# The start, one pair's Gram products and the last square root of a streaming-encoder block on Trainium2

## The chip, the cores and the metric

The kernel runs on one core of one Trainium2 chip. Time is device time in microseconds of that core, from launch to end; the profiled execution also has a span, from its first to its last instruction. Five engines matter: TensorE (PE, and PEld for its weight loads), VectorE (DVE), ScalarE (ACT), GpSimd (POOL) and SyncE (SP), which only issues transfers. Each runs its own list of instructions in order and waits for the others by semaphores.

## The reference

512 frames of 2048 features, ahead of them 16 learned meta tokens, pass one block. An RMS norm and one input projection `P = hn @ w_in` (2048 columns to 8320) feed two groups: sixteen heads of an RWKV-7 recurrence, and a gated convolution of width 3. Both are gated, put together, multiplied by `w_out` and added to the input; a last RMS norm gives the output.

```python
hn = _rmsnorm(h_res, norm_in_g[l])
P = hn @ w_in[l]
...
w_raw = -jax.nn.softplus(-(w0[l] + jnp.tanh(wl) @ w_lora_up[l])) - 0.5
decay = jnp.exp(-jnp.exp(w_raw.astype(jnp.float32)))
...
S = (S * w_t[:, :, None, :] - sa[..., None] * b_t[:, :, None, :]
     + v_t[..., None] * k_t[:, :, None, :])
y_t = jnp.einsum('bhvk,bhk->bhv', S, r_t)
...
h_res = h_res + mix @ w_out[l]
out = _rmsnorm(h_res, norm_f_g)
```

## The kernel before, in words

**Precision.** A product of float32 matrices is made of three matmul passes. Each operand is cut into a high part of reduced width (`xh`, `hi`) and the rest (`xl`, `lo`): high by high, high by rest, rest by high. ScalarE makes the high part (a cast or a scaled copy), VectorE or POOL subtracts it to get the rest. So each 128x512 piece of weights costs a cast (L134) and a subtraction (L135) before TensorE can use it, and each 128-row block of x costs the same with the norm's gain folded in (`split_x`, L207 and L208).

**The projection.** `plan` lists 65 column tiles of `w_in`: lora, k, r, v, g, and for the convolution B, C, h, gc. Features lie on the 16 blocks of 128 partitions (`kt`), and frames are the matmul's columns, 528 of them in two banks of PSUM (256 and 272; 258 where only the 512 real frames and two before them are wanted; one bank of 512 for B and gc). A main matmul is one pass of one block into one bank (L328).

**The head.** Nothing can start before the first weights and the first block of x have come. So the first four tiles (lora, k, r, B) are computed side by side, block by block: for each of the first four blocks (a step) TensorE goes through lora, k, r and B. For this the host packs one array, `front`, in the order in which the pieces are used; four transfers bring it (L237). The first holds the gain, lora's weights of block 0 and block 0 of x; the second k, r and B of block 0; the third the four weights and x of block 1; the fourth blocks 2 and 3. Later loads follow on the same SP queue: the second half of the first weights (`load_w`, L221), then x in groups (`load_x`, L201). A transfer waits until one of eight semaphore lanes is free, so at most eight are under way. Scratch tiles of later stages serve as landing places (`in_bt`, `in_r`, `in_bk`, `in_gt`). Before the first data come, TensorE multiplies zeros (`pwarm`, L187: two float32 matmuls of 512 columns, each of which shows as two passes).

**Fillers.** TensorE's list is written out by hand. `mains()` is a generator that issues the main matmuls of the plan, and everything else calls `fill(ns)` to draw that much main work between two of its own groups, so that the answers of other engines and of transfers come back while TensorE does main work. The numbers are in the table `FW`. `later(ns, ...)` puts a transfer into the list when that much main work has been drawn. The other engines' lists come from a scheduler, except in stretches marked as manual (the head on VectorE and ScalarE, and the end).

**Pairs.** Two heads form a pair; `prepare(i)` handles pair i, and two pairs at a time go through `invert`. In `prepare`, `gram` (L682) multiplies keys by queries for each of nine chunks of frames; the results stand in PSUM as `za` (chunks 0 to 3), `zc` (4 to 7) and `ze` (chunk 8), one bank for each head. `za` lies in the pool `tz`, `zc` in `misc` and `ser`, and `ze` in the pool `main`, which the main matmuls use too. `masked` (L692) multiplies each bank by a mask on VectorE into `gt`, and thereby frees the bank. After a fill (`gram2`) come the sums `n2` and `zb` (L713 to L717). `recur` then goes through the nine chunks; its operands come back from DRAM as `ct` (`load_chunk`), and its first matmuls are `rz` (L957). The fill ahead of it is `begin`.

**The end.** The output projection works with sums of blocks of the mix (units P, M, Q, L1242). Its last unit, M2 of the second half, is done in three pieces: 512 columns for rows 0 to 127, and two of 256 for rows 128 to 255 (L1449). For each 128 rows the sum of squares is collected by ScalarE (L1229, then a read of the accumulator), `row_scale` makes the factor from it, and `finish` scales and stores. The factor is (sum + eps) to the power -0.5: an addition and then a power on POOL (L98). `finish_last(1)` handles the last rows on three engines at once.

Of the kernel before, what the change touches and what calls it, by code (L numbers as in the profile page):

```python
# [9 lines left out]
F32 = mybir.dt.float32  # L10
# [3 lines left out]
ALU = mybir.AluOpType  # L14
# [30 lines left out]
    tr=3200, lev=3000, cp=4200, out=1500, begin=20300, p=2900, u=2900, s=4800, last=3700, mix=2600,  # L45
# [32 lines left out]
def hymba_kernel(ctx: ExitStack, tc: tile.TileContext, xt, xtok, front, w_in, w_out, pv, lup, cst, msk, gf, out):  # L78
# [104 lines left out]
    cold = tp.tile([P, 512], F32, tag="tm", name="cold", bufs=3)  # L183
    nc.vector.memset(cold, 0.0)
    pwarm = pi.tile([P, 512], F32, tag="ser", name="pwarm")
    for _ in range(2):
        nc.tensor.matmul(pwarm, cold[:, 0:P], cold, start=True, stop=True)  # L187
# [17 lines left out]
    def split_x(kt, cols=slice(0, L)):  # L205
        gain = ng[:, kt : kt + 1]
        nc.scalar.activation(xh[:, kt, cols], raw[kt][:, cols], AF.Copy, scale=gain)  # L207
        return nc.vector.scalar_tensor_tensor(  # L208
            out=xl[:, kt, cols], in0=raw[kt][:, cols], scalar=gain, in1=xh[:, kt, cols].bitcast(F32),
            op0=ALU.mult, op1=ALU.subtract,  # L210
        ).ins

    def square_x(kt, first=False):
        sq = accd if first else tr(f"sqx{kt}")[:, 0:L]
        nc.scalar.activation(sq, raw[kt], AF.Square)
        if not first:
            nc.vector.tensor_tensor(out=accd, in0=accd, in1=sq, op=ALU.add)
# [12 lines left out]

    for n in range(4):
# [3 lines left out]
    o = 0  # L235
    for t in fr:
        nc.sync.dma_start(t, front[:, o : o + t.shape[1]])  # L237
        o += t.shape[1]
    ng = fr[0]
    raw[0], raw[1] = fr[0][:, KT + P : F0], fr[2][:, 4 * P : F1]  # L240
    for k in range(2):
        raw[2 + k] = fr[3][:, 8 * P + k * L : 8 * P + (k + 1) * L]
# [3 lines left out]
    nc.scalar.activation(warm, warm, AF.Tanh)  # L246
# [4 lines left out]
    with tc.manual_schedule(engines={mybir.EngineType.DVE, mybir.EngineType.Activation}):  # L251
        split_piece(0, 0, fr[0][:, KT : KT + P])
        split_x(0, slice(0, L // 2))
        split_x(0, slice(L // 2, L))
        for n in (1, 2, 3):
            split_piece(n, 0, fr[1][:, (n - 1) * P : n * P])
        split_x(1)
        for n in range(4):
            split_piece(n, P, fr[2][:, n * P : (n + 1) * P])
        for kt in (2, 3):  # L260
            split_x(kt)
            if kt == 2:
                for n in range(4):
                    split_piece(n, 2 * P, fr[3][:, 2 * n * P : 2 * (n + 1) * P])
# [48 lines left out]
    HALF = SEQ // 2  # L313
# [169 lines left out]
    def mains():  # L483
# [5 lines left out]
        for k in range(4):  # L489
            for n, (ps, rg) in enumerate(four):  # L490
                if k == n == 0:
                    hi, lo = quarters[0]
                    for ww, xx, first in ((hi, xh, True), (lo, xh, False), (hi, xl, False)):
                        for p, (a, b) in zip(ps, rg):
                            nc.tensor.matmul(p, ww[:, 0:P], xx[:, 0, a:b], start=first, stop=False)
# [131 lines left out]
    def prepare(i):  # L627
# [799 lines left out]
    with tc.manual_schedule(engines={mybir.EngineType.DVE, mybir.EngineType.Activation, mybir.EngineType.Pool}):  # L1427
# [3 lines left out]
        for t in (2, 3):  # L1431
            row_part(t, 3)
            row_scale(t, 3)
        row_part(0, 3)
# [25 lines left out]
        row_scale(1, 4, nc.vector)  # L1460
        gain(1, 2, nc.vector, slice(256, 512))
        finish_last(1)


def _layout(i):
# [35 lines left out]
    front += [t[:, 1] for t in first] + [xt[:, 1]] + [t[:, 2:4].reshape(P, 256) for t in first] + [xt[:, 2], xt[:, 3]]  # L1501
# [24 lines left out]
```

## Time and profile before

| | us |
|---|---|
| median of the runs (3; 999.9 to 1000.47) | 1000.18 |
| the profiled execution | 999.89 |
| its span | 998.0 |
| TensorE busy | 986.7 |
| VectorE busy | 689.2 |
| ScalarE busy | 412.2 |
| POOL busy | 271.6 |
| first real matmul (L495) starts | 4.63 |
| last group of matmuls (L1449) ends | 990.1 |

In rows of the order of time the first number is the start in us from the start of the span, the second the duration; then come engine, line, operation, what is written from what, shape and count, and in brackets idle time of the engine before it and what ended it. In rows of a tile the three numbers are the shortest, the median and the longest duration in ns. Matmuls overlap in their pipeline, so the distance between two starts says more than a duration. The loads of data are 139 MB read from HBM over the span, and the data engines are close to full in the first 25 us.

### The profile page before, as it was taken

The page shows a single profiled execution, that of the slowest core. Times are in us where ns is not written, and L with a number is a line of the kernel's source. Part 1 is how long each engine was busy: PE and PEld are TensorE (multiplying, and loading weights), DVE is VectorE, ACT ScalarE, POOL GpSimd, SP SyncE. Part 2 cuts the span into 40 slices and gives each one's busy share as a digit, 9 for nine tenths or more (in the row PEclk, how much of TensorE's full clock was granted, in tenths as well). Part 3 has the DMA queues.
Part 4 walks back from the last instruction along what each step waited for, and adds up shares of the span by engine and source line. Part 5 has one row for each costly group of instructions (what it writes and reads, how often), then busy time and mean ns, then how long its engine had stood idle before and what let it go on. Part 6 is the DMA issues. An engine that isn't in the chain of part 4 may idle for free.

```text
span 998.0 us, 22792 instructions
## 1 busy us (share of the span) xinstructions
PE 986.7 (99%) x9211; PEld 910.8 (91%) x9211; DVE 689.2 (69%) x1314; ACT 412.2 (41%) x770; POOL 271.6 (27%) x286
## 2 busy tenths in 40 slices
PE   9999999999999999999999999999999999999996
PEld 8999999999998999998999998989889898888885
DVE  7777975487774579735579735246555598999895
ACT  7554432343523535232534232233332326645553
POOL 0122423133422324222324222223242423011001
PEclk9999999999999999999999999999999999999999
DMA  9527585437584365854265954978783698798634
GB/s 324 160 79 184 122 224 144 119 106 179 128 215 140 95 180 130 230 145 111 85 180 120 232 143 114 347 266 283 223 266 96 169 266 232 230 293 224 144 99 168
DMA packets 184985, 179.48 MB, mean 180 GB/s; under 512 B 112176, under 2 KB 141616, under 8 KB 184368
## 3 DMA queue, kind: packets, MB, share of 16 engines
q1 hardware_dynamic: 182288, 169.12, 58.2%
q0 software_dynamic: 2304, 8.39, 4.8%
q8 instruction: 72, 1.18, 0.5%
q10 hardware_dynamic: 288, 0.52, 0.1%
q14 instruction: 33, 0.27, 0.1%
HBM read 139.28 MB, written 38.71 MB: 178 GB/s over the span
## 4 chain that ended last, share of the span: by engine, by line
PE 95%; DMA 2%; DVE 1%; issue 1%; POOL 0%; ACT 0%; DVEq 0%; SPq 0%; POOLq 0%
PE ps_g L328 9%; PE ps_r L328 9%; PE ps_h L328 9%; PE ps_gc L328 9%; PE ps_B L328 9%; PE ps_v L328 9%; PE ps_C L328 8%; PE ps_k L328 8%; PE M L1242 8%; PE P L1242 4%; PE Q L1242 2%; PE g L682 2%; DMA ct<-opd 1%; PE ps_lora L328 1%; PE rz L957 1%; PE zs L1004 1%
## 5 line engine op out<-in xcount | busy, mean ns | idle before, releaser
L134 ACT CAST w<-wr 128x512 fp32r<-128x512 f32 x252 | 153.4, 619 | 280.0 <-PE ps_h L328 47.4
L135 POOL TENSOR_TENSOR w<-wr,w 128x512 fp32r<-128x512 f32 x119 | 168.2, 1415 | 365.2 <-ACT w L134 326.7
L135 DVE TENSOR_TENSOR w<-wr,w 128x512 fp32r<-128x512 f32 x133 | 98.3, 743 | 98.6 <-ACT w L134 97.6
L328 PE MATMUL ps_r<-xh,w 128*128 128x256 f32 (+1 forms) x512 | 95.2, 282 | 1.0 <-DVE gt L692 1.0
L328 PE MATMUL ps_k<-xh,w 128*128 128x256 f32 (+1 forms) x512 | 95.4, 284 | 0.0
L328 PE MATMUL ps_v<-xh,w 128*128 128x272 f32 (+1 forms) x512 | 95.4, 284 | 0.0
L328 PE MATMUL ps_h<-xh,w 128*128 128x258 f32 (+1 forms) x512 | 93.1, 281 | 0.0
L328 PE MATMUL ps_C<-xh,w 128*128 128x258 f32 (+1 forms) x512 | 92.5, 281 | 0.0
L328 PE MATMUL ps_g<-xh,w 128*128 128x258 f32 (+1 forms) x512 | 91.7, 280 | 0.0
L328 PE MATMUL ps_B<-xh,w 128*128 128x512 f32 x256 | 83.1, 394 | 0.0
L328 PEld LDWEIGHTS ps_r<-xh,w 128*128 128x128 f32 x512 | 80.2, 189 | 1.6 <-DVE gt L692 1.2
L328 PE MATMUL ps_gc<-xh,w 128*128 128x512 f32 x256 | 81.6, 393 | 0.0
L328 PEld LDWEIGHTS ps_k<-xh,w 128*128 128x128 f32 x512 | 80.3, 189 | 0.3
L328 PEld LDWEIGHTS ps_v<-xh,w 128*128 128x128 f32 x512 | 80.1, 189 | 0.3
L328 PEld LDWEIGHTS ps_h<-xh,w 128*128 128x128 f32 x512 | 79.5, 189 | 0.3
L328 PEld LDWEIGHTS ps_C<-xh,w 128*128 128x128 f32 x512 | 79.2, 189 | 0.6
L328 PEld LDWEIGHTS ps_g<-xh,w 128*128 128x128 f32 x512 | 79.2, 189 | 0.2
L328 PE MATMUL ps_k<-xl,w 128*128 128x256 f32 (+1 forms) x256 | 73.0, 285 | 0.0
L328 PE MATMUL ps_v<-xl,w 128*128 128x256 f32 (+1 forms) x256 | 72.5, 283 | 0.0
L328 PE MATMUL ps_h<-xl,w 128*128 128x256 f32 (+1 forms) x256 | 72.5, 283 | 0.0
L328 PE MATMUL ps_g<-xl,w 128*128 128x256 f32 (+1 forms) x256 | 72.4, 283 | 0.0
L328 PE MATMUL ps_r<-xl,w 128*128 128x256 f32 (+1 forms) x256 | 72.1, 282 | 0.0
(312 smaller groups left out, 2204.3 us busy)
## 6 DMA issues: line engine op xcount, KB each, us to landing
wr<-in_w_in_dram SPq DMA_DIRECT2D x126, 512.0 KB
ct<-opd SPq DMA_DIRECT2D x56, 320.0 KB
wo<-in_w_out_dram SPq DMA_DIRECT2D x21, 512.0 KB
opd<-gt SPq DMA_DIRECT2D x16, 576.0 KB
x<-in_w_out_dram POOLq DMA_DIRECT2D x16, 512.0 KB, 5.7
opd<-ar SPq DMA_DIRECT2D x8, 576.0 KB
opd<-bt SPq DMA_DIRECT2D x64, 64.0 KB
ct<-opd SPq DMA_DIRECT2D x16, 256.0 KB
```

Of the source, the lines that this page charges most:

```text
L134: nc.scalar.copy(hi, rq)
L135: low[q] = eng.tensor_tensor(out=lo, in0=rq, in1=hi.bitcast(F32), op=ALU.subtract).ins
L328: nc.tensor.matmul(ps[r], ww[:, w], xx[:, kt, a:b], start=(kt == 0 and n == 0), stop=(kt == KT - 1 and n == 2))
L682: nc.tensor.matmul(z[h][:, c - c0], bk[hs, c, h : h + 2, :].rearrange("p a s -> p (a s)"), ar[hs, c].rearrange("p a s -> p (a s)"), start= ...
L957: nc.tensor.matmul(z[e][ho if e else hs, 0, k], ct[e][hs, k, o : o + CH], uv(e, k, hs, h) if part else st[hs, 4 * e + k], start=(part == 0 ...
L1004: nc.tensor.matmul(zs[hs, j], bb[:, h], uv(e, k, everything, h), start=True, stop=True)
L1242: nc.tensor.matmul(bank[s], left(prod, jj, m, s), w, start=(jj == 0 and n == 0), stop=(jj == 7 and n == 2))
```

## The change

Five things change.

1. Warming: four matmuls of 128 columns instead of two of 512, on a tile of 128 columns.
2. The front: five transfers instead of four. The first holds the gain, lora's weights and the first 256 columns of block 0 of x; the second the other 272 columns and the weights of k, r and B; then one transfer for each of blocks 1, 2 and 3. The landing places of the first two change (`in_r` for the first, `in_bt` for the second). The fourth and all later loads are held until the first has landed: POOL copies one column from it into the fourth's landing place. Lora's cast of block 0 goes from ScalarE to VectorE, and lora's six passes go by part of x (three passes into the first bank, three into the second) instead of by kind of pass.
3. Gram: for pair 2 chunk 8 comes first, on TensorE as in the masks' program order; for other pairs nothing moves.
4. Two fills are longer: `gram2` of pair 1 by 400 ns and `begin` by 500 ns.
5. The factor of the last rows is a square root on ScalarE and a reciprocal on VectorE; a square root of one unused element stands earlier on ScalarE, so that the table is loaded there. Rows 128 to 255 have their last product with the final gain moved ahead of it.

The first instructions of TensorE, before and after (`ps_lora` has two numbered banks; `w` is the weight slot):

```order
L187 MATMUL pwarm<-cold 128x512 x2
L495 MATMUL ps_lora_331<-xh,w_143 128x256
L495 MATMUL ps_lora_332<-xh,w_143 128x272
L495 MATMUL ps_lora_331<-xh,w_143 128x256
L495 MATMUL ps_lora_332<-xh,w_143 128x272
L495 MATMUL ps_lora_331<-xl,w_143 128x256
L495 MATMUL ps_lora_332<-xl,w_143 128x272
L328 MATMUL ps_k_0_333<-xh,w_144 128x256
```

After:

```order
L187 MATMUL pwarm<-cold 128x128 x4
L506 MATMUL ps_lora_344<-xh,w_145 128x256 x2
L506 MATMUL ps_lora_344<-xl,w_145 128x256
L506 MATMUL ps_lora_345<-xh,w_145 128x272 x2
L506 MATMUL ps_lora_345<-xl,w_145 128x272
L339 MATMUL ps_k_0_346<-xh,w_146 128x256
```

The bank of the second 272 columns is now used only after the first bank is through. SP's first loads, before and after:

```order
L237 DMA in_bt<-in_front_dram 128x672
L237 DMA in_r_148<-in_front_dram 128x384
L237 DMA in_bk<-in_front_dram 128x1040
L237 DMA in_gt_150<-in_front_dram 128x2080
L221 DMA in_g<-in_w_in_dram 128x512
L201 DMA in_gt_157<-in_xt_dram 128x2112
```

After; the fourth waits for POOL, and the others stand behind it:

```order
L242 DMA in_r_150<-in_front_dram 128x400
L242 DMA in_bt<-in_front_dram 128x656
L242 DMA in_bk<-in_front_dram 128x1040
L242 DMA in_gt_149<-in_front_dram 128x1040 x2
L222 DMA in_g<-in_w_in_dram 128x512
L201 DMA in_gt_162<-in_xt_dram 128x2112
```

The first three transfers carry the same 2096 columns, cut at another place. VectorE at pair 2, around the masks (`g2_8_0` is chunk 8 of the first head, `g2_0_1` chunks 0 to 3 of the second):

```order
L821 STREAM_TRANSPOSE vs2_3136<-v2_2781 128x576
L135 TENSOR_TENSOR w72_2858<-wr36_2856,w72_2858 128x512
L692 TENSOR_TENSOR gt2_2919<-g2_0_0_2920,cs_119 128x512
L692 TENSOR_TENSOR gt2_2919<-g2_0_1_2921,cs_119 128x512
L692 TENSOR_TENSOR gt2_2919<-g2_4_0_2922,cs_119 128x512
L692 TENSOR_TENSOR gt2_2919<-g2_8_0_2924,cs_119 128x128
L692 TENSOR_TENSOR gt2_2919<-g2_4_1_2923,cs_119 128x512
L692 TENSOR_TENSOR gt2_2919<-g2_8_1_2925,cs_119 128x128
L352 TENSOR_TENSOR pr_k3_2969<-ps_k3_0_2801,rs_112 128x256
```

After:

```order
L836 STREAM_TRANSPOSE vs2_3153<-v2_2794 128x576
L135 TENSOR_TENSOR w72_2871<-wr36_2869,w72_2871 128x512
L703 TENSOR_TENSOR gt2_2936<-g2_8_0_2941,cs_119 128x128
L703 TENSOR_TENSOR gt2_2936<-g2_8_1_2942,cs_119 128x128
L703 TENSOR_TENSOR gt2_2936<-g2_0_0_2937,cs_119 128x512
L703 TENSOR_TENSOR gt2_2936<-g2_0_1_2938,cs_119 128x512
L703 TENSOR_TENSOR gt2_2936<-g2_4_0_2939,cs_119 128x512
L703 TENSOR_TENSOR gt2_2936<-g2_4_1_2940,cs_119 128x512
L363 TENSOR_TENSOR pr_k3_2982<-ps_k3_0_2814,rs_112 128x256
```

The two small masks move from the fourth and sixth place to the first two. The diff, with the parts left out that only follow from it:

```diff
-    tr=3200, lev=3000, cp=4200, out=1500, begin=20300, p=2900, u=2900, s=4800, last=3700, mix=2600,
+    tr=3200, lev=3000, cp=4200, out=1500, begin=20800, p=2900, u=2900, s=4800, last=3700, mix=2600,
...
-    cold = tp.tile([P, 512], F32, tag="tm", name="cold", bufs=3)
+    cold = tp.tile([P, P], F32, tag="tm", name="cold", bufs=3)
...
-    for _ in range(2):
-        nc.tensor.matmul(pwarm, cold[:, 0:P], cold, start=True, stop=True)
+    for _ in range(4):
+        nc.tensor.matmul(pwarm, cold, cold, start=True, stop=True)
...
-    F0, F1, F2 = KT + P + L, 4 * P + L, 8 * P + 2 * L
-    fr = [view("bt", F0), view("r0", 3 * P), view("bk", F1), view("gt0", F2)]
+    F0, F1 = KT + P + HALF, 4 * P + L
+    X0 = L - HALF
+    two = view("gt0", 2 * F1)
+    fr = [view("r0", F0), view("bt", X0 + 3 * P), view("bk", F1), two[:, 0:F1], two[:, F1 : 2 * F1]]
...
+    for n in range(3):
+        load_front(n)
...
+    nc.scalar.activation(warm, warm, AF.Tanh)
+    nc.gpsimd.tensor_copy(fr[3][:, 0:1], ng[:, 0:1])
+    load_front(3)
+    load_front(4)
...
-        split_piece(0, 0, fr[0][:, KT : KT + P])
-        split_x(0, slice(0, L // 2))
-        split_x(0, slice(L // 2, L))
+        hi, lo = (t[:, 0:P] for t in quarters[0])
+        w0 = fr[0][:, KT : KT + P]
+        nc.vector.tensor_copy(hi, w0)
+        nc.vector.tensor_tensor(out=lo, in0=w0, in1=hi.bitcast(F32), op=ALU.subtract)
+        for cols, t in x0:
+            split_x(0, cols, t)
...
-                    for ww, xx, first in ((hi, xh, True), (lo, xh, False), (hi, xl, False)):
-                        for p, (a, b) in zip(ps, rg):
+                    for p, (a, b) in zip(ps, rg):
+                        for ww, xx, first in ((hi, xh, True), (lo, xh, False), (hi, xl, False)):
...
-        for c in range(NCH):
-            gram((za, zc, ze)[c // 4], c, c // 4 * 4)
-        for z, a, b in ((ze, 8, 9), (za, 0, 4), (zc, 4, 8)) if i == 2 else ((za, 0, 4), (zc, 4, 8), (ze, 8, 9)):
+        blocks = [(za, 0, 4), (zc, 4, 8), (ze, 8, 9)]
+        if i == 2:
+            blocks = blocks[2:] + blocks[:2]
+        for z, a, b in blocks:
+            for c in range(a, b):
+                gram(z, c, a)
+        for z, a, b in blocks:
             masked(z, a, b)
-        fill(FW["gram2"] - shift + 1300 * (i == 1) + 2000 * (i == 3))
+        fill(FW["gram2"] - shift + 1700 * (i == 1) + 2000 * (i == 3))
...
+        if eng is nc.scalar:
+            eng.activation(v, ssq[:, t, n : n + 1], AF.Sqrt, bias=w)
+            nc.vector.reciprocal(r, v)
+            scales[t] = r
+            return
...
+        nc.scalar.activation(fv[:, 1, 1:2], fv[:, 3, 0:1], AF.Sqrt)
...
-        row_scale(1, 4, nc.vector)
         gain(1, 2, nc.vector, slice(256, 512))
+        row_scale(1, 4, nc.scalar)
         finish_last(1)
```

More of the change, by code (lines that the diff above doesn't have):

```diff
@@ L214, in square_x @@
         sq = accd if first else tr(f"sqx{kt}")[:, 0:L]
-        nc.scalar.activation(sq, raw[kt], AF.Square)
+        for cols, t in ((slice(0, L), raw[kt]),) if kt else x0:
+            nc.scalar.activation(sq[:, cols], t, AF.Square)
         if not first:
@@ L245, in hymba_kernel @@
     later_w += [load_w(1, "xT1"), load_w(2, "e1"), load_w(3, "xT0")]
-    nc.scalar.activation(warm, warm, AF.Tanh)
     load_x("ar", 8, 2)
@@ L261, in hymba_kernel @@
             split_x(kt)
-            if kt == 2:
-                for n in range(4):
-                    split_piece(n, 2 * P, fr[3][:, 2 * n * P : 2 * (n + 1) * P])
+            for n in range(4):
+                split_piece(n, kt * P, fr[kt + 1][:, n * P : (n + 1) * P])
         split_w(1, later_w[0], nc.vector)
@@ L1500, in _layout @@
     front = [pv[:, V_NG : V_NG + KT], first[0][:, 0], xt[:, 0]] + [t[:, 0] for t in first[1:]]
-    front += [t[:, 1] for t in first] + [xt[:, 1]] + [t[:, 2:4].reshape(P, 256) for t in first] + [xt[:, 2], xt[:, 3]]
+    for k in range(1, 4):
+        front += [t[:, k] for t in first] + [xt[:, k]]
     front = np.concatenate(front, 1)
```

29 lines of the change are left out of this document (14 added, 15 removed).

## The prediction

> **What bounds the kernel now.** I read the page first (busy times and the chain), then the waits of TensorE, then the order of time at the four places that the change touches. TensorE is busy almost throughout, and the chain that ended last is TensorE for 95 parts in 100.
>
> ```profile
> PE 986.7 (99%) x9211; PEld 910.8 (91%) x9211; DVE 689.2 (69%) x1314; ACT 412.2 (41%) x770; POOL 271.6 (27%) x286
> PE 95%; DMA 2%; DVE 1%; issue 1%; POOL 0%; ACT 0%; DVEq 0%; SPq 0%; POOLq 0%
> ```
>
> So an engine beside TensorE is worth something only where TensorE waits for it, and what stands behind TensorE's last matmul. The longest wait in the waits view, after the 1.4 for the very first memset, is this; the next is 0.3:
>
> ```profile
> PE ps_r L328 <- DVE gt L692: 1.0, 1, 1.0
> ```
>
> A wait of TensorE that goes moves the end by its length, since nothing else holds TensorE between the head and its last matmul. "Busy" hides one thing: at the head TensorE is busy with warming and with matmuls that stretch. The head in order of time (start, duration):
>
> ```profile
> 0.73 0.39 SPq L237 DMA_DIRECT2D in_bt<-in_front_dram  x1
> 0.73 1.28 ACT L246 ACT_TABLE_LOAD   x1 [0.73 <-PEq L1513]
> 2.03 0.20 ACT L246 ACTIVATE warm<-warm 128x1 f32<-128x1 f32 x1
> 3.86 0.30 ACT L227 CAST w<-in_bt 128x128 fp32r<-128x128 f32 x1 [1.63 <-DMA in_bt<-in_front_dram]
> 4.06 0.92 ACT L207 ACTIVATE xh<-in_bt 128x264 fp32r<-128x264 f32 x2
> 4.61 0.90 DVE L208 SCALAR_TENSOR_TENSOR xl<-in_bt,xh 128x264 fp32r<-128x264 f32 x2
> 4.63 0.69 PE L495 MATMUL ps_lora<-xh,w 128*128 128x256 f32 x1
> 4.89 0.68 ACT L227 CAST w<-in_r 128x128 fp32r<-128x128 f32 x3
> 5.79 0.28 PE L328 MATMUL ps_k<-xh,w 128*128 128x256 f32 x1
> 7.12 0.74 ACT L207 ACTIVATE xh<-in_bk,in_bt 128x528 fp32r<-128x528 f32 x1 [1.55 <-DMA in_bk<-in_front_dram]
> 7.68 0.40 PE L328 MATMUL ps_B<-xh,w 128*128 128x512 f32 x1
> 8.10 0.38 PE L328 MATMUL ps_lora<-xh,w 128*128 128x256 f32 x1
> 8.71 0.39 PE L328 MATMUL ps_lora<-xl,w 128*128 128x256 f32 x1 [0.23 <-DVE xl L208]
> 11.41 0.40 PE L328 MATMUL ps_B<-xh,w 128*128 128x512 f32 x1
> 11.65 0.28 PE L328 MATMUL ps_lora<-xh,w 128*128 128x256 f32 x1
> 14.52 0.28 PE L328 MATMUL ps_lora<-xh,w 128*128 128x256 f32 x1
> ```
>
> One 128-row block of x (lora, k, r and B of it: a step) takes 14.52 - 11.65 = 2.87 us when nothing waits. Counted back from 11.65, the second step would have begun at 8.78 had it run without a wait. The first step was done at 7.91: its last pass began at 7.68, and the next matmul follows such a pass after 11.65 - 11.41 = 0.24. So 0.87 us of the head is the wait for the third transfer (in_bk), and before 5.79 lie the wait for the first data, the warming and lora's six passes.
>
> **The change part by part.** *First transfer.* It falls from 672 to 400 columns, from 344 to 205 KB. What the transfers moved (last number: GB/s, so KB in a microsecond):
>
> ```profile
> 1.00:2.00 1.00, 0.55 (x1) 0.50 (x2) 0.39 (x1) 1.00 (x1) 1.00 (x6) 1.00 0.30 35
> 2.00:3.00 1.00, 1.00 (x2) 0.34 (x1) 0.00 (x0) 0.22 (x2) 0.26 (x2) 1.00 0.82 253
> 3.00:4.00 1.00, 1.00 (x2) 0.34 (x1) 0.00 (x0) 0.14 (x1) 0.00 (x0) 1.00 1.06 378
> 4.00:5.00 1.00, 1.00 (x3) 0.29 (x1) 0.68 (x2) 1.00 (x4) 0.00 (x0) 1.00 0.94 383
> ```
>
> 139 KB less is 0.37 us at 378 GB/s and 0.55 at 253; I take 0.45, so ScalarE can begin at 3.41. The weight's cast goes to VectorE, xh's first half (0.46, half of the row at 4.06) is ready at 3.87, and the first matmul stands there instead of at 4.63. The passes now go by part of x: the second part comes with the second transfer, which ends with the same bytes as before: 197 KB more at 378 GB/s is 0.52 after 3.86, 4.38, and no later than 4.89, when its casts begin now. From 4.4: xh 0.46, xl 0.45, so lora's last pass begins at 5.31 and k at 5.43. k, r and B take 7.91 - 5.79 = 2.12, so the first step ends at 7.55 (8.04 by the late end). Their casts and subtractions, 0.23 each, run ahead of them as they do now.
>
> *Third transfer.* The first three are 1073 KB as before; the rows above moved 1049 KB by 5.00, so 5.06 is the early end of its landing and 7.12, the row as it is, the late one. It now has no later load in flight beside it. The first transfer's 344 KB had been moved by 3.15 and were used at 3.86, 0.7 later, so I take 5.06 + 0.7 = 5.8. The second step's xl pass ran 8.71 - 7.12 = 1.6 after the landing: 7.4, just in time for 7.55. The gain of the head is then 8.78 - 7.55 = 1.23; with a little lost at that seam I take 1.1. Its ends are 0 (landing at 7.1) and 1.3.
>
> *Warming.* Eight passes of 128 columns instead of four of 512.
>
> ```profile
> L187 PEld LDWEIGHTS pwarm<-cold x4: 288/335/337, 1.4 to 3.3; 128*128 128x128 f32 x4
> L187 PE MATMUL pwarm<-cold x4: 1034/1061/1222, 1.4 to 4.2; 128*128 128x512 f32 x4
> ```
>
> Four passes started from 1.4 to 4.2, 0.9 apart; a quarter of that is 0.23, and eight take 1.8, or 2.7 by the 0.335 of a weight load. They end between 3.3 and 4.1, at or before the first data, where today's last pass (4.2) still runs when the matmul of 4.63 is due. The shorter memset ahead of them only lets them begin earlier, off the path. The price is idle TensorE before the first data and between lora's parts: rival 2.
>
> *Later loads held back.* POOL copies one column when the first transfer has landed (I take the 0.2 of ScalarE's one-column row), and the fourth load waits for that; behind it in SP's queue stand the fifth and all later ones. Behind the copy POOL has only memsets of tiles that are first used after the projections. The fourth issue comes at 3.6; its bytes begin about 1 us after the issue, as the first transfer's did (0.73, and 35 KB in the second microsecond), at 4.6, before the first three are through at 5.06. So the engines that move data have no gap.
>
> ```profile
> 9.67 0.74 ACT L207 ACTIVATE xh<-in_gt,in_bt 128x528 fp32r<-128x528 f32 x1 [1.02 <-DMA in_gt<-in_front_dram]
> 14.24 2.81 DVE L208 SCALAR_TENSOR_TENSOR xl<-in_gt,in_bt,xh 128x528 fp32r<-128x528 f32 x4 [0.41 <-ACT xh L207]
> 18.55 0.28 PE L328 MATMUL ps_lora<-xl,w 128*128 128x256 f32 x1
> ```
>
> The fourth load is half as large, so the third step, now due at 7.55 + 2.87 = 10.4, no longer waits for the fourth step's bytes (9.67 now). The next quarter of x has its last xl at 17.05, used at 18.55: 1.5 to spare, of which the earlier head uses 1.1; 0.4 is left for a later landing. The smaller pieces add four casts and four subtractions, about 0.2 of new time each, and one more square; they lie beside TensorE's 2.87 a step: nothing.
>
> *Gram of pair 2.* VectorE's masks of this pair now begin with the two small ones, of chunk 8, which free the bank for ps_r; they stood fourth and sixth.
>
> ```profile
> L692 DVE TENSOR_TENSOR gt<-g,cs x6: 273/674/678, 218.0 to 220.6; 128x512 f32<-128x512 f32 x4, 128x128 f32<-128x128 f32 x2
> 218.74 0.28 PE L328 MATMUL ps_k<-xl,w 128*128 128x272 f32 x1
> 218.87 0.29 PE L328 MATMUL ps_k<-xh,w 128*128 128x272 f32 x1
> 220.11 0.38 PE L328 MATMUL ps_r<-xh,w 128*128 128x256 f32 x1 [0.96 <-DVE gt L692]
> ```
>
> Matmuls follow at 0.13, so ps_r was due at 219.0 and is 1.1 late. Two small masks of 0.27 from 218.0 end at 218.55, and at 218.95 if the 0.4 us of the longer fill moves them too: still in time. Gain 1.0 (ends 0.7 and 1.1). The large masks are then 0.5 later; they are read by the pair's next sums, which stand behind 5.5 us of fill.
>
> *The two fill numbers.* 0.4 us more of main matmuls stands before pair 1's sums, 0.5 more before the recurrence.
>
> ```profile
> 130.21 0.29 PE L714 MATMUL n_tz<-sq_l,ones 128*2 128x288 f32 x1
> 130.63 0.47 PE L716 MATMUL zb<-rk_h,ones 128*128 128x512 f32 x1
> 630.97 0.81 PE L957 MATMUL rz<-ct 64*64 64x64 f32 x28
> 632.11 0.33 PE L957 MATMUL rz<-ct 64*64 64x64 f32 x4 [0.33 <-DMA ct<-opd]
> ```
>
> zb starts 0.42 after a pass that is 0.13 to 0.29 long: 0.13 to 0.3 lost, 0.2 taken. The last four rz matmuls start 1.14 after the first 28, which took 0.81: 0.33, as the row has it; 0.3 taken. Half a microsecond more of work ahead covers either. No matmul is added; those drawn forward are missing behind.
>
> *Square root at the end.* Today VectorE adds, POOL raises to a power, and three engines wait:
>
> ```profile
> 990.98 0.19 ACT L1229 ACTIVATION_READ_ACCUMULATOR sqj<-xb 128x1 f32 x1
> 992.19 0.72 ACT L1420 ACTIVATE xa<-xa,fv 128x512 f32<-128x512 f32 x1 [1.02 <-POOL fv L98]
> 979.01 0.63 ACT L1229 ACTIVATE sqj_None<-xb 128x512 f32<-128x512 f32 x1 [1.07 <-DVE xb L1223]
> 987.27 0.42 DVE L1453 TENSOR_TENSOR xb<-xb,end 128x256 f32<-128x256 f32 x1 [0.92 <-PE end L1449]
> ```
>
> Then it is a one-column pass on ScalarE (0.20) and one on VectorE (0.2 too) with two handovers of 0.1: 0.6 instead of 1.02, a gain of 0.4 (ends 0 and 0.6). It also puts a table load (1.28) and a one-column pass on ScalarE ahead of the square at 979.01. They fall into 1.07 of idle time, so some 0.5 sticks out, and what follows is 0.5 later up to 987.27; there VectorE waits 0.92 for TensorE, which takes it up. Without that cover it would cost 0.5.
>
> The sum: 1.1 + 1.0 + 0.2 + 0.3 + 0.4 = 3.0 us. The profiled execution took 999.89 (span 998.0), so 996.9; the median of the runs shown is 0.29 above it, so 997.2 against 1000.18.
>
> **The rivals.**
> 1. The third transfer is still late. For it: one execution alone shows the landing, and what held it from 5.06 to 7.12 need not be the later loads. Head 0.1, sum 2.0: 998.2.
> 2. TensorE starts slowly. For it: the first real matmul took 0.69, the same form later 0.28, and warming's passes stood 0.9 apart. With TensorE idle in part of the first 5 us, k, r and B could run at half their pace, up to 2.12 more: the head is 0.9 worse than now, not 1.1 better, and the sum 1.0: 999.2. Against it: 1.8 to 2.7 of warming and lora's first passes still fill most of the time up to 5. [...]
> 3. The held loads come too late for the second quarter: were it later by the whole 1.5 us of the issue, 1.1 would be a stall, the sum 1.9: 998.3. Against it: the engines have bytes until 5.06.
> 4. The displaced groups meet one new wait like pair 2's, 1.0: 998.2, or two: 999.2.
> 5. Slower: in the recurrence all groups stand 0.4 us later against the main matmuls. If a bank is then late in every chunk, as one was at pair 2, eight chunks give the gain back from 0.4 us each and end slower by 0.2% from 0.63 each (5.0 in all): 1002.2 and more. Against it: after 632 no wait of TensorE is listed.
>
> **How the numbers follow.** Chances: forecast 0.48 (own range 996.0 to 998.1), rivals 0.17, 0.16, 0.06, 0.07 and 0.06. 0.2%, 2.0 us, is about what a measurement of this kernel can tell from no change: faster means under 998.18. There lie the forecast, half of rivals 1, 3 and 4 and a fifth of 2, which may be milder: 0.66. Slower is rival 5, 0.06; the same has 0.28. The range goes from the good ends of head, gram and end (1.3, 1.1 and 0.6 for 1.1, 1.0 and 0.4 give 996.7; the runs' own spread of 0.6 leads to 996.0) to rival 2 (999.4).
>
> **What would show it.** The first real matmul near 3.9 and k near 5.4; the third transfer used before 6 and the second step begun near 7.6; no wait of ps_r for gt at pair 2 and none of rz for ct; 0.6 from the last accumulator read to the scaling. Wrong it would be by matmuls of k and r that last 0.5 after 5.4, or by a new row among TensorE's waits.

## The result, and the profile after

The changed kernel takes 998.43 us (median of 22 runs, 997.36 to 1000.81) against 1000.12 (22 runs, 998.8 to 1001.37): a ratio of 0.9986, with a 95% interval of 0.998 to 0.9992. A second series on another occasion (the first experiment of the third group below) gave 0.998 (0.9971 to 0.9988). So it is faster by 1.4 to 2.0 us, where 3.0 were forecast; the median lies above 998.18, the bound under which the prediction would have called the kernel faster. The profiled execution took 998.27, with a span of 996.5 (999.89 and 998.0 before).

The page of the kernel after: its first row of busy times, and its chain by engine.

```profile
PE 986.2 (99%) x9215; PEld 913.0 (92%) x9215; DVE 688.2 (69%) x1319; ACT 413.8 (42%) x777; POOL 267.6 (27%) x286
PE 98%; DVE 1%; DMA 0%; ACT 0%; issue 0%; DVEq 0%; ACTq 0%
```

TensorE's busy time hardly differs; what it waits for does. The waits of TensorE after (total, times, longest, in us):

```profile
PE pwarm L187 <- DVE cold L184: 1.0, 1, 1.0
PE ps_lora L506 <- DVE w L265: 0.7, 1, 0.7
PE tz L582 <- DVE xT L934: 0.3, 1, 0.3
PE prs L491 <- DVE rs L489: 0.2, 1, 0.2
```

ps_r's wait of 1.0 at pair 2, rz's for ct and the one at z are gone. Three rows are new: 0.7 before the first real matmul, 0.3 for `tz`, pair 2's low rank product, which waits for VectorE's copies out of the same pool, and 0.2 for `prs`, which waits for a copy on VectorE. The head after, in order of time:

```profile
1.05 2.08 PE L187 MATMUL pwarm<-cold 128*128 128x128 f32 x8 [1.05 <-DVE cold L184]
3.31 0.51 ACT L208 ACTIVATE xh<-in_r 128x256 fp32r<-128x256 f32 x1 [1.09 <-DMA in_r<-in_front_dram]
3.88 0.80 PE L506 MATMUL ps_lora<-xh,w 128*128 128x256 f32 x2 [0.75 <-DVE w L265]
4.31 0.52 ACT L208 ACTIVATE xh<-in_bt,in_r 128x272 fp32r<-128x272 f32 x1 [0.48 <-DMA in_bt<-in_front_dram]
5.81 0.41 PE L339 MATMUL ps_k<-xh,w 128*128 128x256 f32 x1
6.03 0.41 PE L339 MATMUL ps_k<-xl,w 128*128 128x256 f32 x1
6.56 0.74 ACT L208 ACTIVATE xh<-in_bk,in_r 128x528 fp32r<-128x528 f32 x1 [1.15 <-DMA in_bk<-in_front_dram]
8.41 0.63 PE L339 MATMUL ps_B<-xh,w 128*128 128x512 f32 x1
8.84 0.63 PE L339 MATMUL ps_B<-xl,w 128*128 128x512 f32 x1
9.27 0.49 PE L339 MATMUL ps_B<-xh,w 128*128 128x512 f32 x1
9.60 0.28 PE L339 MATMUL ps_lora<-xh,w 128*128 128x256 f32 x1
11.75 0.39 PE L339 MATMUL ps_B<-xh,w 128*128 128x512 f32 x1
11.98 0.40 PE L339 MATMUL ps_B<-xl,w 128*128 128x512 f32 x1
12.45 0.28 PE L339 MATMUL ps_lora<-xh,w 128*128 128x256 f32 x1
```

The data come as forecast: ScalarE starts on the first at 3.31 and on the second at 4.31, and the first real matmul stands at 3.88. The warming is through at 3.1, though, so TensorE is idle for 0.75. Then see the pace, that is the distance between the starts of two passes of one size: 5.81 to 6.03 is 0.22 for 256 columns, 8.41 to 8.84 is 0.43 for 512; two steps later 11.75 to 11.98 is 0.23 for 512. The same passes take nearly twice as long until about 9.4. So the second step begins at 9.60 instead of the forecast 7.6, with its data there since 6.56, and the third at 12.45, 0.80 later than before (11.65).

Further on, the waits that were to go are gone. VectorE's masks at pair 2, with ps_k's last pass and ps_r's first behind it; and the first rz matmuls:

```profile
218.32 2.87 DVE L703 TENSOR_TENSOR gt<-g,cs 128x128 f32<-128x128 f32 x6
219.44 0.29 PE L339 MATMUL ps_k<-xh,w 128*128 128x272 f32 x1
219.57 0.28 PE L339 MATMUL ps_r<-xh,w 128*128 128x256 f32 x1
630.94 0.69 PE L972 MATMUL rz<-ct 64*64 64x64 f32 x32
```

ps_r follows after 0.13 instead of 1.24, and the 32 rz matmuls run in one piece. The end after:

```profile
989.39 0.19 ACT L1244 ACTIVATION_READ_ACCUMULATOR sqj<-xb 128x1 f32 x1
989.61 0.29 ACT L1415 ACTIVATE fv<-ssq,fv 128x1 f32<-128x1 f32 x1
989.95 0.16 DVE L1416 RECIPROCAL fv<-fv 128x1 f32<-128x1 f32 x1
990.14 0.72 ACT L1440 ACTIVATE xa<-xa,fv 128x512 f32<-128x512 f32 x1 [0.24 <-DVE fv L1416]
991.66 0.34 ACTq L1445 DMA_DIRECT2D out_dram<-xb  x1
```

From the accumulator's read to the scaling it is 0.75, where it was 1.21. But from that read to the end of the span it is 996.5 - 989.39 = 7.11, where it was 998.0 - 990.98 = 7.02.

Where the time went, in the two profiled executions (TensorE's last matmul starts at 988.23 instead of 989.83):

| place | forecast gain | measured |
|---|---|---|
| head (start of the third step) | 1.1 | -0.80 |
| ps_r at pair 2 | 1.0 | 1.1 |
| zb | 0.2 | 0.29 |
| rz | 0.3 | 0.54 |
| z (178.7 before) | none | 0.38 |
| tz (196.4 after, new) | none | -0.42 |
| steps too small to list | none | 0.5 |
| the end, behind the last matmul | 0.4 | -0.1 |
| sum | 3.0 | 1.5 |

The middle rows are by the distance of two starts over the usual one, which is more than the wait that the waits view shows. The row of small steps is what is left of the 1.6 by which TensorE's last matmul is earlier; no instruction is named for it.

### The profile page after: what moved, and what is told of

It reads as the page before. It is cut to its first block, busy times and chain, and to the rows that moved or that the text cites. A ratio compares the mean times of both kernels' runs of the same rounds, so it can differ in the third digit from the quotient of the medians.

```text
span 996.5 us, 22816 instructions
## 1 busy us (share of the span) xinstructions
PE 986.2 (99%) x9215; PEld 913.0 (92%) x9215; DVE 688.2 (69%) x1319; ACT 413.8 (42%) x777; POOL 267.6 (27%) x286
## 4 chain that ended last, share of the span: by engine, by line
PE 98%; DVE 1%; DMA 0%; ACT 0%; issue 0%; DVEq 0%; ACTq 0%
PE ps_k L339 9%; PE ps_h L339 9%; PE ps_r L339 9%; PE ps_C L339 9%; PE ps_g L339 9%; PE ps_gc L339 9%; PE ps_v L339 9%; PE ps_B L339 9%; PE M L1257 8%; PE P L1257 4%; PE Q L1257 2%; PE g L693 2%; PE ps_lora L339 1%; PE rz L972 1%; PE zs L1019 1%; PE zy L1023 1%
## 5 line engine op out<-in xcount | busy, mean ns | idle before, releaser
L339 PE MATMUL ps_C<-xl,w 128*128 128x256 f32 (+1 forms) x256 | 72.0, 281 | 0.0
```

The costliest lines, as they stand in the source:

```text
L339: nc.tensor.matmul(ps[r], ww[:, w], xx[:, kt, a:b], start=(kt == 0 and n == 0), stop=(kt == KT - 1 and n == 2))
```

## The experiments, first group: the parts alone, and longer warming

Two theories stood against each other. P: TensorE's pace; idle time behind the short warming keeps the passes at the long distance. L: the loads; the third transfer was used at 6.56 instead of 5.8.

**Twelve warming passes.** The changed kernel, with

```diff
-    for _ in range(4):
+    for _ in range(6):
         nc.tensor.matmul(pwarm, cold, cold, start=True, stop=True)
```

> The changed kernel with twelve warming passes of 128 columns in place of eight; nothing else. Theory P (TensorE's pace): the eight passes end at 2.95 us, TensorE stands idle until 3.88, and the passes of k, r and B then follow each other at 0.21 us instead of 0.12 until about 9.4; with no idle time they come to 0.12 some 2 to 4 us earlier, at half the pace that is 1.0 to 1.5 us: 997.1 us (996.7 to 997.5) against 998.4 for the changed kernel, the second step at 7.8 to 8.5 us instead of 9.6. Theory L (the loads: the third transfer is used at 6.56 instead of the forecast 5.8, and that is where the gain of the head went): warming moves no load, so 998.4 as the changed kernel, the second step still after 9 us.

Measured: 997.78 us against 999.89 before in the same group, a ratio of 0.9979 (0.997 to 0.9988). Its head:

```profile
1.05 2.93 PE L187 MATMUL pwarm<-cold 128*128 128x128 f32 x12 [1.05 <-DVE cold L184]
3.85 0.79 PE L506 MATMUL ps_lora<-xh,w 128*128 128x256 f32 x2
7.25 0.40 PE L339 MATMUL ps_B<-xh,w 128*128 128x512 f32 x1
7.49 0.40 PE L339 MATMUL ps_B<-xl,w 128*128 128x512 f32 x1
7.96 0.28 PE L339 MATMUL ps_lora<-xh,w 128*128 128x256 f32 x1
11.07 0.28 PE L339 MATMUL ps_lora<-xh,w 128*128 128x256 f32 x1
```

The hole (the idle time between the warming and the first real matmul) is filled; B's passes are 0.24 apart instead of 0.43; the second step begins at 7.96 and the third at 11.07, 1.38 earlier than in the changed kernel. The third transfer was used at 6.55 here too. Nothing but four passes of zeros was added, so P holds for the head and L falls. The time itself, 997.78, is above the 996.7 to 997.5 that was expected, and its interval overlaps that of the changed kernel (0.998 to 0.9992). In this profile most of the 1.38 is lost again late: at 859 to 872 TensorE waits for VectorE, 1.1 in all by the distances, and the last matmul is only 0.26 earlier. The largest of these waits, and in the same kernel two successive POOL issues of an accumulating load into `x`, a tile that VectorE's work there reads:

```profile
870.88 2.35 PE L1257 MATMUL M<-o,S 128*128 128x512 f32 x9 [0.47 <-DVE o L1230]
836.20 0.86 POOL L1216 DMA_DIRECT2D x<-in_w_out_dram  x1 [3.92 <-DVE w L135]
846.23 0.89 POOL L1216 DMA_DIRECT2D x<-in_w_out_dram  x1 [9.17 <-ACT S L1187]
```

They are 10.0 us apart here and 7.7 in the changed kernel. Whether these issues are the cause was not tried. The earlier head is not enough to explain the loss: in the five other profiles of this document with a loss there it was 0.1 to 0.4, and in three of these TensorE came 0.2 to 0.6 earlier to that place than here.

**Warming and front alone.**

The kernel before, with eight warming passes of 128 columns, the five front transfers, POOL's copy and lora's passes by part of x.

> The kernel before with the warming and the front of the change; Gram order, fills and end as before. Theory P: the second step begins at 9.6 us where the kernel before would have begun it at 8.8 without its wait, so slower by 0.6 (0 to 1.2): 1000.7 us against 1000.1. Theory L: a head that gains the 0.1 of rival 1: 1000.0. The forecast's own term: 999.0. The wait of 0.3 at L582 in the changed kernel (tz for VectorE's copies of xT) shows here if the shifted head causes it, and not if the longer fills do.

Measured: 999.46, ratio 0.9995 (0.9987 to 1.0004): no change that these runs can tell, where theory P had expected 1000.7. The profile has the slow head (second step at 9.79, third at 12.66, 1.01 later than before), and yet TensorE's last matmul is 0.20 earlier than before. Its waits at z and rz are gone, as if the fills had been made longer. The reading is that these two groups wait for work that does not come later with the head, so that a late head only shortens their waits; for z the profile names nothing that the group waits for, and no run tests it. There is no wait at tz, so that one comes from the longer fill of pair 1.

**Gram order and fills alone.**

```diff
-    ... begin=20300, ...
+    ... begin=20800, ...
...
+        blocks = [(za, 0, 4), (zc, 4, 8), (ze, 8, 9)]
+        if i == 2:
+            blocks = blocks[2:] + blocks[:2]
...
-        fill(FW["gram2"] - shift + 1300 * (i == 1) + 2000 * (i == 3))
+        fill(FW["gram2"] - shift + 1700 * (i == 1) + 2000 * (i == 3))
```

> The kernel before with the Gram order of pair 2 and the two longer fills alone. Both theories: ps_r's wait of 1.12 at pair 2 gone, zb's 0.28 and rz's 0.54 gone: 1.9 us, less 0.4 if the new wait at tz comes from the fills: 998.2 to 998.6 us against 1000.1. The forecast had 1.5 for the three: 998.6.

Measured: 997.96, ratio 0.9978 (0.9969 to 0.9987); 1.9 less. tz's wait of 0.3 is there, and for that case 998.6 was expected. Set beside the changed kernel, instruction by instruction, TensorE's work stands 1.1 earlier from the third step on, and this difference stays between 1.0 and 1.1 to the last matmul. With the waits at z and rz gone, a late head is no longer taken up by anything. By this reading the parts do not add: the head alone cost nothing, and beside the fills it costs 1.0 in these two executions. The medians of the runs put it at 0.5 (998.43 against 997.96), and their intervals overlap.

**The end alone.**

```diff
+        if eng is nc.scalar:
+            eng.activation(v, ssq[:, t, n : n + 1], AF.Sqrt, bias=w)
+            nc.vector.reciprocal(r, v)
...
+        nc.scalar.activation(fv[:, 1, 1:2], fv[:, 3, 0:1], AF.Sqrt)
...
-        row_scale(1, 4, nc.vector)
         gain(1, 2, nc.vector, slice(256, 512))
+        row_scale(1, 4, nc.scalar)
```

> The kernel before with the square root and reciprocal at the end alone. The forecast's term: 0.4 less, 999.7 us against 1000.1, with the scaling 0.6 to 0.75 us after the last accumulator read (1.21 before). Rival: the last transfer's landing eats it, as in the one profile of the changed kernel, where the last issue came 0.28 earlier after TensorE's last matmul but the span ended 0.1 later: 1000.1, no change.

Measured: 1000.0, ratio 1.0002 (0.9993 to 1.0012): no change that these runs can tell. The scaling and the last issue in its profile:

```profile
990.99 0.19 ACT L1229 ACTIVATION_READ_ACCUMULATOR sqj<-xb 128x1 f32 x1
991.74 0.72 ACT L1425 ACTIVATE xa<-xa,fv 128x512 f32<-128x512 f32 x1 [0.24 <-DVE fv L1401]
993.10 0.33 SPq L1429 DMA_DIRECT2D out_dram<-xa  x1
```

0.75 from read to scaling, and 2.11 from read to last issue (2.56 before). The span of 997.8 ends 6.8 after the read, against 7.0 before: 0.2 of the 0.45 arrives here, and in the changed kernel nothing, where ScalarE's last issue came 2.27 after the read. Over all fourteen profiles of this document, the time from the start of TensorE's last matmul to the end of the span is 8.00 to 8.38 in the nine with the new end (mean 8.16) and 8.12 to 8.20 in the five with the old one (mean 8.18).

## The experiments, second group: one piece at a time

**The shorter warming alone.**

```diff
-    cold = tp.tile([P, 512], F32, tag="tm", name="cold", bufs=3)
+    cold = tp.tile([P, P], F32, tag="tm", name="cold", bufs=3)
...
-    for _ in range(2):
-        nc.tensor.matmul(pwarm, cold[:, 0:P], cold, start=True, stop=True)
+    for _ in range(4):
+        nc.tensor.matmul(pwarm, cold, cold, start=True, stop=True)
```

> The kernel before with the shorter warming alone (eight passes of 128 columns). Theory P (TensorE's pace): TensorE stands idle from about 3.0 to 4.5, so its passes stay at the long distance (0.21 us for 256 columns) until 8 to 11; the third step begins at 12.0 to 13.2, where three profiles with the old warming have 11.3 to 11.7. The head-only kernel, 1.0 later at its third step, had the waits at z and rz (1.1 together) no longer, so of the 0.5 to 1.7 most comes back: 999.9 to 1000.8 us against 999.9. Theory L (the pace does not hang on the warming): third step at 11.3 to 11.7, 999.9.

Measured: 1000.12 against 1000.03, ratio 1.0001 (0.9992 to 1.0009).

```profile
1.05 2.07 PE L187 MATMUL pwarm<-cold 128*128 128x128 f32 x8 [1.05 <-DVE cold L184]
4.58 1.44 PE L495 MATMUL ps_lora<-xh,w 128*128 128x256 f32 x4 [1.46 <-ACT xh L207]
8.87 0.46 PE L328 MATMUL ps_B<-xh,w 128*128 128x512 f32 x1
9.63 0.28 PE L328 MATMUL ps_lora<-xh,w 128*128 128x256 f32 x1
12.51 0.28 PE L328 MATMUL ps_lora<-xh,w 128*128 128x256 f32 x1
```

With the old front the first matmul is at 4.58 as before, and the hole of 1.46 makes the third step begin at 12.51 instead of 11.65. So the slow head is the work of the warming and not of the front. All of the 0.86 is given back further on, where the waits at z and rz are gone; the last matmul is 0.1 earlier than before.

**The Gram order of pair 2 alone.**

```diff
-        for c in range(NCH):
-            gram((za, zc, ze)[c // 4], c, c // 4 * 4)
...
+        blocks = [(za, 0, 4), (zc, 4, 8), (ze, 8, 9)]
+        if i == 2:
+            blocks = blocks[2:] + blocks[:2]
+        for z, a, b in blocks:
+            for c in range(a, b):
+                gram(z, c, a)
...
```

> The kernel before with the Gram order of pair 2 alone, the fills as they were. As forecast (1.0 for this term): ps_r's wait of 1.1 at pair 2 gone and nothing in its place: 998.8 us against 999.9; zb's 0.28, z's 0.4 and rz's 0.5 stay and no wait stands at tz (pair 2's low rank product), so the rest of the Gram-and-fills kernel's 1.9 is the fills' work. Rival: the large masks, now later, hold the pair's next sums for 0.5: 999.4.

Measured: 999.07 against 1000.03, ratio 0.9991 (0.9982 to 0.9999): 1.0, the forecast's figure. The wait of ps_r is gone, those at zb (0.28), z (0.26) and rz (0.55) stay, and there is none at tz. The rest of the first group's 1.9 is then the fills': about 1.0 by the medians instead of the forecast 0.5, though the intervals of the two kernels overlap. In the profiles the longer fill of pair 1 brings little (zb and z gained, tz lost), and the 0.5 of `begin` brings the more: rz's wait, and a wait of 0.33 in a later chunk of the recurrence (683 us), which the kernel with the Gram order alone has, and neither the one with the fills nor the kernel before.

**Without the hold.** The kernel with twelve passes, less

```diff
-    nc.gpsimd.tensor_copy(fr[3][:, 0:1], ng[:, 0:1])
```

> The changed kernel with twelve warming passes (997.8 us) without POOL's copy, so that the fourth and later loads are issued at once. If the hold is worth what the forecast said: the third transfer is used at about 7.1 instead of 6.5, the second step's pass with the rest of x at 8.7 instead of 8.14, 0.5 slower: 998.3. Rival: the third transfer's bytes come no later without the hold, second step as it was: 997.8.

Measured: 998.67, ratio 0.9987 (0.9978 to 0.9996).

```profile
3.30 0.51 ACT L208 ACTIVATE xh<-in_r 128x256 fp32r<-128x256 f32 x1 [1.08 <-DMA in_r<-in_front_dram]
5.03 0.52 ACT L208 ACTIVATE xh<-in_bt,in_r 128x272 fp32r<-128x272 f32 x1 [1.22 <-DMA in_bt<-in_front_dram]
7.82 0.74 ACT L208 ACTIVATE xh<-in_bk,in_r 128x528 fp32r<-128x528 f32 x1 [1.68 <-DMA in_bk<-in_front_dram]
```

The third transfer was used at 7.82, and in the other profiles without a hold at 6.10 to 7.62; in all seven with the hold at 6.46 to 6.66. The means are 0.65 apart, and the scatter is gone with the hold. But six of the seven without it have the old front, cut otherwise; with the same front there is this one profile, so the size of what the hold brings is not shown. Here the second transfer too came late, at 5.03 (it did so once with the hold, at 5.11, in the next kernel); TensorE stood idle for 0.64 between lora's halves, and in spite of twelve warming passes the third step began at 12.82. So a hole between lora's halves did the same here as one ahead of the first matmul, and the 998.67 is the work of this hole as much as of the third transfer.

**500 ns more fill ahead of pair 2's low rank product.** The kernel with twelve passes, and

```diff
-        fill(FW["out"] if first < NPAIR - 2 else FW["begin"])
+        fill(FW["out"] + 500 * (first == 0) if first < NPAIR - 2 else FW["begin"])
```

> The changed kernel with twelve warming passes and 500 ns more fill after the first inversion, ahead of pair 2's low rank product. The wait of tz for VectorE's copies of xT (0.42 us, new with the longer fill of pair 1) goes: 997.4 us against 997.8. Rival: moving the main matmuls against pair 2's groups brings another wait there of 0.4 or more: 997.8 or later.

Measured: 996.5 (5 runs, 995.98 to 996.95), ratio 0.9967 (0.9954 to 0.9979). The wait at tz is gone and none has come there. The gain on the kernel with twelve passes, 1.3 between two series, is larger than the 0.42 of that wait; this kernel's profile lost 0.4 at 859 to 872, the other's 1.1.

## The experiments, third group: side by side

**The changed kernel again**, without an edit.

> The changed kernel once more, beside the next three on one chip. Theory P (after the idle time behind the short warming TensorE comes to full pace at some time between 7.3 and 10.7 us, another in each run): third step at 11.4 to 13.1 us, time 998.4, runs spread over more than 2 us. Rival (12.45 was one odd execution): third step at 11.1 to 11.3, and the runs no wider than those of the kernel with twelve passes.

Measured: 998.48, ratio 0.998 (0.9971 to 0.9988). Third step at 12.50. The runs span 1.5 us (997.25 to 998.78, 11 runs), not the more than 2 expected, though the 22 of the first series span 3.4.

**The best so far again**, twelve passes and the 500 ns.

> The changed kernel with twelve warming passes and 500 ns more fill ahead of pair 2's low rank product, once more. Theory P: full pace before 7.9 us unless the second transfer leaves a hole, third step at 10.9 to 11.6, no wait at tz: 996.5 to 997.4 us, 1.0 to 1.9 below the changed kernel in this call. Rival (the first result, of five runs, was luck, and only the 0.4 at tz is real): 0.4 below the changed kernel.

Measured: 996.58 (5 runs, 996.4 to 998.0), ratio 0.9967 (0.9954 to 0.9979), 1.9 below the changed kernel. Its third step begins at 10.98, 1.5 earlier than in the run above; with the 0.4 at tz that is the 1.9. Its waits of TensorE, less the first memset's:

```profile
PE ps_lora L506 <- ACT xh L208: 0.3, 1, 0.3
PE prs L491 <- DVE rs L489: 0.2, 1, 0.2
```

**The old head with all the rest.**

The kernel above, with four warming passes of 512 columns, the four front transfers and lora's passes by kind of pass.

> Gram order, fills, end and the 500 ns of the kernel above, but the head of the kernel before (four passes of 512 columns, four front transfers). By the third steps seen so far (11.3, 11.3, 11.7 and 11.9 with the old head, 11.1 and 11.5 with the new front and twelve passes) the new front is worth 0.3 where TensorE is at pace: 0.3 slower than the kernel above, about 997.0 to 997.5. By the forecast's term for the head: 1.1 slower.

Measured: 997.13 (7 runs), ratio 0.997 (0.9959 to 0.9981): 0.55 above the kernel with the new front, between the 0.3 and the 1.1; the intervals overlap. By the medians the new front with twelve warming passes is worth about half a microsecond, which these runs cannot tell from nothing. The changed kernel, measured beside it, is 1.35 slower than this old head with the same gains further on (by the medians; the intervals overlap a little), and 0.4 of that is tz.

**Four passes of zeros between lora's halves.** The best so far, and

```diff
+                        if p is ps[0]:
+                            for _ in range(2):
+                                nc.tensor.matmul(pd[0][:, 0:P], cold, cold, start=True, stop=True)
```

> The kernel above with the new head and four more passes of zeros between the two halves of lora's first step, where TensorE waited 0.2 to 1.2 us for the second transfer. Theory P: idle time is what keeps the pace down, so full pace before 7.9 us in the profile and in nearly every run; where the second transfer comes in time the four passes cost up to 0.7: about the same median, a narrower spread, 996.3 to 997.2. Rival (idle time of this length does not matter): the passes only delay, k starts 0.5 later than the 5.7 to 6.5 seen and the median is 0.4 to 0.7 above the kernel without them.

Measured: 996.59 (5 runs, 995.62 to 997.19), ratio 0.9962 (0.9948 to 0.9975): as the kernel without them.

```profile
4.66 0.61 PE L510 MATMUL ps_B<-cold 128*128 128x128 f32 x4
7.81 0.28 PE L339 MATMUL ps_lora<-xh,w 128*128 128x256 f32 x1
11.05 0.28 PE L339 MATMUL ps_lora<-xh,w 128*128 128x256 f32 x1
```

They cost nothing to be seen here, since the second half's data were not there before 4.9. Whether they narrow the spread cannot be said from five runs.

## Why the prediction was right and wrong

The direction held, and 998.4 lies in the stated range of 996.0 to 999.4. It lies there only by the part that was added for the rivals: the forecast's own range ended at 998.1. The size did not hold: 1.5 in the profile (1.4 to 2.0 by the runs) instead of 3.0. The head missed its term by 1.9 and the end by 0.5; the other terms and the steps that were not foreseen gave 0.9 back, which is luck.

- **Warming, costed at "off the path"; it failed.** The step took the end of the warming "between 3.3 and 4.1, at or before the first data", and the shorter memset as something that "only lets them begin earlier". It lets them end earlier too: eight passes from 1.05 ended at 3.1, and the first matmul, which needs the data's cast, came at 3.88, where the prediction itself had put it. The hole of 0.75 is what rival 2 described, with k, r and B "at half their pace" and a head "0.9 worse than now"; measured, passes of 256 columns 0.22 apart where they are 0.12 apart from 9.60 on, and a head 0.80 worse. That rival had a chance of 0.16; its total of 999.2 was 0.8 too late, because the fills gave more than forecast. Its listed counterargument, that warming and lora's first passes "fill most of the time up to 5", was the wrong measure: with 0.75 of it left empty, filling most of it was not enough here.
- **First transfer.** ScalarE at 3.41, second part at 4.4, first matmul 3.9: measured 3.31, 4.31, 3.88. The six lora passes at the slow pace then ate the lead, k came at 5.81 instead of 5.43, as before the change.
- **Third transfer, forecast at 5.8.** It was used at 6.56, 0.8 later. The transfers moved 314 and 349 GB/s between 3 and 5 us instead of the 378 and 383 that were assumed, and 295 in the microsecond after that; an estimate from these rows is that the 1073 KB were through at about 5.4, and the use came 1.2 after that instead of 0.7; why is not shown. It cost nothing in the changed kernel, where TensorE was not ready for it before 9.60. With twelve passes and the hold it cost the second step 0.2 at most.
- **Later loads held back, costed at nothing.** No cost is seen: the fourth load was issued at 3.61 (forecast 3.6), and the fourth block of x was not waited for. What the hold brings is not measured by itself, as said above.
- **Gram of pair 2, 1.0.** Right to a tenth, alone and in the whole.
- **The two fills, 0.2 and 0.3.** Too small by the profile, 0.29 and 0.54; together about 1.0 by the medians of the kernels without the other parts. Two things were not foreseen: z's wait goes too, and pair 1's longer fill makes a new wait of 0.4 at tz, of the kind that rival 4 had, at less than half its size.
- **Square root at the end, 0.4.** The step to the scaling gained 0.46, more than forecast. What failed was taking it through to the end: behind it the last transfers have to be issued and landed, and nothing arrives that fourteen profiles or the runs can tell (8.16 against 8.18 from the last matmul to the end of the span).
- **Rival 5** (a late bank in every chunk) did not come: no wait of TensorE after 632 is listed.

Of the table load, 0.5 was to stick out, and VectorE's wait of 0.92 for TensorE was to take it up. Nothing stuck out: the load stands at 975.71, in ScalarE's idle time, and the square behind it at 977.12. That is 1.9 earlier than the 979.01 of before, while TensorE is 1.6 earlier. VectorE's wait is still 0.92 long, at 985.67, so it had nothing to take up.

## What to carry to other kernels

Warming is not done when it has run for some microseconds: here 2.1 us of it with a hole of 0.75 behind it put the first pass at full pace (the short distance) at 9.60, and 2.9 us without a hole at 5.92. In this kernel it had to go on until full pace began, or reach up to the first real matmul without a hole there or further on (0.64 between lora's halves did the same); so its length is set by the moment the first operand is ready, and it has to be lengthened when that moment or the size of the passes changes. A gain at the head may be eaten by a later group that waits for something with a time of its own, and a loss may be taken up there, as all of the 0.86 of the shorter warming alone was: look for such waits first, because they do it in silence, and stop doing so as soon as they are tuned away. And a gain on a chain that ends in transfers is to be read at the landing of the last one: here 0.46 at the scaling was -0.1 at the end of the span.

## What the runs showed of the hardware

The windows view prints a granted clock of 1.00 from the first microsecond, in the kernel before and in the changed one. The distances of the passes show a slower pace at the start all the same: in the changed kernel 0.43 for 512 columns at 8.84 and 0.23 at 11.75, 0.22 for 256 columns at 5.81 and 0.12 at 9.60; the pass at 9.27, 0.33 from the next, lies between the two. What sets the pace is not shown. Below, full pace is the short distance, and a hole is idle time of TensorE between its warming passes and k.

| kernel | holes, us, as listed | first pass at the short distance, us | third step, us |
|---|---|---|---|
| before | none | 5.16 | 11.65 |
| Gram and fills; end; order; old head with the rest | none | 6.32; 5.79; 7.19; not listed | 11.32; 11.34; 11.87; 12.09 |
| twelve passes; with 500 ns (twice); with the bridge | none; 1.0, 0.3; none | 5.92; by 4.7 (both); 4.66 | 11.07; 11.45, 10.98; 11.05 |
| changed (twice); warming and front | 0.75, 1.0; 0.9 | 9.60, not listed; 9.79 | 12.45, 12.50; 12.66 |
| short warming alone; without the hold | 1.5; 0.6 | 9.16; 9.49 | 12.51; 12.82 |

Of the twelve profiles listed, no one with a hole ahead of full pace has a pass at the short distance before 9.16, and none without one has its first later than 7.19. The kernel with the 500 ns had its hole (4.7 to 5.7 in one profile, about 4.7 to 5.0 in the other) after full pace had begun: the last pass ahead of it lasts 0.36 in one and 0.33 in the other, where its like in the changed kernel lasts 0.51 (at 4.47). It kept full pace through the hole: behind it k's first two passes are 0.12 apart in one (6.45) and 0.11 in the other (5.77).

The smallest hole that went with the late pace is the 0.64 of the kernel without the hold. How short a hole may be to do no harm, and what decides the moment of full pace, is not shown.

With unbroken warming the first pass at the short distance stands between 5.16 and 7.19 with the old warming (four profiles) and between 4.7 and 5.92 with twelve passes (four). An estimate from this: at the long distance (0.43 where the short one is 0.23) a delay of 2.0 costs 0.9, so that executions of the kernel before can differ by about 1 us at the head; the third steps seen with the old warming (five profiles) are 11.32 to 12.09.

The moments that the expectations set for full pace (before 7.9 without a hole; 7.3 to 10.7, or 8 to 11, after one) were the author's estimates under theory P. No run shows them as limits; the runs show the first pass at the short distance at 4.7 to 7.19 without a hole ahead of it, and at 9.16 to 9.79 with one.

What stays open: why the kernel with twelve passes alone was 1.3 slower than with the 500 ns, where tz accounts for 0.4; the 1.1 that its one profile lost at 859 to 872, against 0.4, would cover most of the rest, but no run separates the two. Nor is it shown what held ScalarE's last issue in the changed kernel, which comes 3.4 after the start of the last matmul there and 3.1 after it in the kernel with the new end alone.
